# Token sums as products with a column of ones, and scales spread by products with the identity, in a two-block sequence kernel

## The chip, the core and the metric

One NeuronCore of a Trainium2 chip runs the whole program in one launch. The metric is the device time of that launch in microseconds (us), the median of several runs. The kernel before takes 2175.45 us (three runs, 2174.98 to 2176.43). TensorE is called PE below, its weight loads PEld, VectorE DVE, ScalarE ACT and GpSimd POOL; SP issues most DMAs.

## The reference, cut to what matters

Two blocks follow each other on 1024 tokens of 1024 features. The change touches the normalizations only. Each is

```
def rms_norm(x, w):
    xf = x.astype(jnp.float32)
    y = xf * lax.rsqrt(jnp.mean(xf * xf, axis=-1, keepdims=True) + EPS)
    return (y * w.astype(jnp.float32)).astype(x.dtype)
```

and they stand before the first block's input product, before its gate, at its end, before the second block's input product, after its mixer, before its feed-forward part and after it. Besides them a modulation vector `mod = silu(c) @ ada_w + ada_b` of 6 x 1024 numbers is made, by the same sum over partitions.

## The kernel before, in words

Features lie on the 128 partitions, tokens along the free axis, in two halves of H = 512 tokens. Matrix products are done on PE in float32r with each operand split in a high and a low part, so each product of 128 x 128 weights with 512 tokens is three PE instructions (`mm3`). PE's order is the order in which the program is written: `tick` counts the modelled time of these products, and every 2500 ns (640 ns in the feed-forward part) `slot` lets generators on the lists `fast` and `side` take one step, so a `yield` in a generator puts the next PE instructions that many slots later. On DVE, ACT, POOL and SP a scheduler orders the instructions.

A norm is a chain over engines. While the features come out of their products, ACT squares them and DVE adds the eight squares up in an accumulator of 128 x 512 (`acc`). What is left is a sum over the 128 partitions for each token, and a scale for each token that must stand on all partitions.

- `token_sums` (line 2539 before) has PE transpose the accumulator in chunks of 128 tokens into PSUM (one instruction for each chunk, `tr`, line 2478), and DVE sums along the free axis (line 2545). The result is a column for each chunk: token on the partition.
- `rsqrt_cols` (line 2549) scales on DVE and raises to the power -0.5 on POOL (line 2552).
- `to_rows` (line 2554) has DVE multiply the identity by the repeated columns (line 2557, 128 x 512, into a tile `C` or `B`), PE multiplies a 128 x 128 tile of ones with it (one product of 512 float32 columns, two PE instructions), and ACT copies the result out of PSUM.

`token_sums` is called 27 times: twice in phase A (`rstd`), twelve times for the modulation vector (`ada`, line 1557), twice for the gate's norm, four times in `norms` (two norms for each half: the first block's last and the second's first, lines 1710 and 1711), four times in `mid` and three times in `finish` (512, 256 and 256 tokens). That is 104 chunks. `to_rows` is called 15 times, 56 chunks. In `norms` the second scale is computed from the first: `r1`, then `r2` by three small products, a second power and a last product (lines 1712 to 1718). `norms(0)` is followed by the scaling of the second block's inputs (`x1`), which DVE and ACT do between the last drains of the gate products; `mid(1)` makes the feed-forward inputs of the second half while the products of the first half run; `finish` ends the program.

Of the kernel before, what the change touches and what calls it, by code (L numbers as in the profile page):

```python
# [8 lines left out]
F32 = mybir.dt.float32  # L9
# [3 lines left out]
ALU = mybir.AluOpType  # L13
# [3 lines left out]
P = 128  # L17
T = 1024
H = 512
D = 1024  # L20
NCH = T // P
EPS = 1e-6
# [98 lines left out]
class PhaseA:  # L121
# [14 lines left out]
    def phase_a(self):  # L136
        nc, tc = self.nc, self.tc
# [18 lines left out]
        acc = tp.tile([P, NCH * 256], F32, tag="vt", name="acc_a", bufs=1)[:, :T]  # L156
        rb = tp.tile([P, T], F32, tag="rb", name="rb_a")
        rt = sp.tile([P, NCH], F32, tag="rt", name="rt_a")
        rtmp = sp.tile([P, NCH], F32, tag="rtmp", name="rtmp_a")
# [3 lines left out]
        for half in range(2):  # L163
            hs = slice(half * H, half * H + H)
# [24 lines left out]
        def rstd(half):  # L189
            hs = slice(half * H, half * H + H)  # L190
            hr = slice(half * 4, half * 4 + 4)
            self.token_sums(rt[:, hr], acc[:, hs])
            self.rsqrt_cols(rt[:, hr], rt[:, hr], 1.0 / D, EPS, rtmp[:, hr])
            yield
            yield
            self.to_rows(rb[:, hs], rt[:, hr], 4)
# [24 lines left out]
        for k in range(8):  # L221
            first_k(p0, 0, k)
        p1 = {j: self.sm_ps() for j in range(3)}
        chain = rstd(0)
        for k in range(8):
            first_k(p1, 1, k)
            if k in (1, 4, 6):
                next(chain, None)
        for j in range(4):
            drain(p0[j], first[j], 0)  # L230
        p1[3] = self.mm_ps()
        chain = rstd(1)
        for k in range(8):
            first_k({3: p1[3]}, 1, k)
# [1293 lines left out]
class PhaseC:  # L1528
# [11 lines left out]
    def ada(self, g, half, pool):  # L1540

        o = g * 1024 + half * H
        for k in range(8):
            raw = pool.tile([P, H], F32, tag="adar", name=self.name("adar"), bufs=2)
            self.nc.sync.dma_start(raw, self.a["adaw"][k * P : k * P + P, o : o + H])
            if k == 0:
                acc = pool.tile([P, H], F32, tag="adaa", name=self.name("adaa"), bufs=1)
                self.ts(acc, raw, self.cact[:, 0:1])
            else:
                self.stt(acc, raw, self.cact[:, k : k + 1], acc, ALU.mult, ALU.add)  # L1550
            if k % 2:
                yield
        yield
        yield
        j = g * 8 + half * 4
        m = self.mods[:, j : j + 4]
        self.token_sums(m, acc)
        self.add(m, m, self.col("ada_b_2", j, 4))

    def halves(n, head, tail):  # L1560

# [12 lines left out]
    def rstd_rows(self, sums, col, tmp, rows, lag=3, res=None):  # L1574

        n = sums.shape[1] // P
        self.token_sums(col, sums)
        self.rsqrt_cols(col, col, 1.0 / D, EPS, tmp)
        for _ in range(lag):
            yield  # L1580
        r = self.to_rows(rows, col, n)
        if res is not None:
            res.append(r)

    def phase_c(self, yh, yl):
        nc, tc = self.nc, self.tc
        tp = tc.alloc_tile_pool(name="tc", bufs=1, side="left")
        sp = tc.alloc_tile_pool(name="tcs", bufs=1, side="left")
        br = self.br = tc.alloc_tile_pool(name="bridge", bufs=1, side="right")
# [5 lines left out]
        def B_():  # L1595
            return br.tile([P, H], F32, tag="B", name=self.name("B"), bufs=3)
# [3 lines left out]
        def pair(pool, n):  # L1600
            return [pool.tile([P, H], F32, tag=f"{n}{j}", name=self.name(n)) for j in range(2)]
# [9 lines left out]
        acc, rb = pair(tp, "acc"), pair(tp, "rb")  # L1611
        rt = br.tile([P, NCH], F32, name="rt_c")
        rtmp = br.tile([P, NCH], F32, name="rtmp_c")
# [50 lines left out]
        for n, (m, half) in enumerate(self.UC[6:]):  # L1664
            ps = self.mm_ps()
# [8 lines left out]
        acc1, acc2 = pair(br, "acc1"), pair(br, "acc2")  # L1674
# [15 lines left out]
            accum(acc2[half], m, hh, scale=self.col("final_norm_w", m))  # L1690


        wfa = br.tile([P, 8], F32, name="wfa")
        r1 = br.tile([P, NCH], F32, name="r1")
        r2 = br.tile([P, NCH], F32, name="r2")
        rb12 = pair(br, "rb12")
        self.x2d = [tc.dram_tile([P, T], F32, name=f"x2d{k}") for k in range(8)]
        x1 = self.x1 = []
# [1 line left out]
        def norms(half):  # L1700
            if not x1:

                self.stt(wfa, self.mods[:, 8:16], 1.0, self.col("pre1_w_2", 0, 8), ALU.add, ALU.mult)
                self.mul(wfa, wfa, self.col("final_norm_w", 0, 8))
                x1.extend(self.moving())
            hs = slice(half * H, half * H + H)
            hr = slice(half * 4, half * 4 + 4)
            for _ in range(4):
                yield
            self.token_sums(r1[:, hr], acc1[half])  # L1710
            self.token_sums(r2[:, hr], acc2[half])
            self.rsqrt_cols(r1[:, hr], r1[:, hr], 1.0 / D, EPS, rtmp[:, hr])
            self.mul(r2[:, hr], r2[:, hr], r1[:, hr])
            self.mul(r2[:, hr], r2[:, hr], r1[:, hr])
            self.rsqrt_cols(r2[:, hr], r2[:, hr], 1.0 / D, EPS, r2[:, hr])
            self.mul(r2[:, hr], r2[:, hr], r1[:, hr])
            yield
            yield
            self.to_rows(rb12[half], r2[:, hr], 4)
            for k in range(8):  # L1720
                t = B_()
                s = self.mods[:, k : k + 1]
                self.stt(t, h[k][:, hs], wfa[:, k : k + 1], rb12[half], ALU.mult, ALU.mult)
                self.act(x1[0][k][half], t, AF.Identity, bias=s)
                self.stt(x1[1][k][half], t, s, x1[0][k][half].bitcast(F32), ALU.add, ALU.subtract)

        def store_x2(half):
            hs = slice(half * H, half * H + H)
            if half == 0:
                for _ in range(4):  # L1730
                    yield
            rb1 = br.tile([P, H], F32, tag=f"acc1{half}", name=self.name("rb1"))
            self.to_rows(rb1, r1[:, half * 4 : half * 4 + 4], 4)
            for k in range(8):
                t = B_()
                self.stt(t, h[k][:, hs], self.col("final_norm_w", k), rb1, ALU.mult, ALU.mult)
                (nc.sync if k % 2 else nc.gpsimd).dma_start(self.x2d[k][:, hs], t)
                yield

        def chain():  # L1740
            yield from norms(1)
            yield from store_x2(0)
            yield from store_x2(1)
# [6 lines left out]
        for m, half in self.UG[6:]:  # L1750
            ps = self.mm_ps()
            self.prod(ps, ws.get(("g", m)), x, half)
            gate_drain(ps, m, half)
            if (m, half) == (7, 0):
                self.drain_side()
                self.fast.append(norms(0))
# [579 lines left out]
class K(PhaseA, PhaseB, PhaseC, PhaseF):  # L2336
# [199 lines left out]
        nc.gpsimd.memset(self.mhalf, -0.5)  # L2536


    def token_sums(self, out, acc):

        n = out.shape[1]
        ps = self.sm_ps()[:, : n * P]
        for j in range(n):
            self.tr(ps[:, j * P : (j + 1) * P], acc[:, j * P : (j + 1) * P])
        self.nc.vector.tensor_reduce(
            out=out, in_=ps.rearrange("p (n c) -> p n c", n=n), axis=mybir.AxisListType.X, op=ALU.add
        )

    def rsqrt_cols(self, out, src, scale, eps, tmp):

# [2 lines left out]

    def to_rows(self, out, colt, n):

        dg = self.C_().rearrange("p (n c) -> p n c", n=4)[:, :n, :]
        self.nc.vector.tensor_tensor(
            out=dg, in0=self.ident.unsqueeze(1).broadcast_to([P, n, P]), in1=colt.unsqueeze(2).broadcast_to([P, n, P]),
            op=ALU.mult,
        )  # L2560
        ps = self.sm_ps()[:, : n * P]
        self.mm(ps, self.ones, dg.rearrange("p n c -> p (n c)"))
        if out is None:
            return ps
        self.act(out, ps, AF.Copy)
# [26 lines left out]
```

## Time and profile before

| what | value |
|---|---|
| median of three runs | 2175.45 us |
| the profiled execution | 2174.98 us, its span 2173.3 us |
| granted clock of PE, mean | 0.994 |
| PE busy | 2127.4 us (98%) |
| DVE busy | 1505.0 us (69%) |
| ACT busy | 904.7 us (42%) |
| POOL busy | 120.5 us (6%) |

The page's busy time of PE holds the modelled ends of pipelined products, so the start of one product to the start of the next is read instead where a cost is wanted. A line of a timeline is: start, length of the merged run, engine, line, operation, result and operands, shape, count, and in brackets the idle time before it with what ended it.

### The profile page before, as it was taken

How to read it: one execution, taken by the hardware profiler on the slowest of the kernel's cores; microseconds unless marked ns; L12 is line 12 of the kernel's file. 1: busy time of each engine (PE TensorE's matmuls, PEld its weight loads, DVE VectorE, ACT ScalarE, POOL GpSimd, SP SyncE). 2: the span in 40 equal slices, each digit the busy share in tenths (PEclk: the TensorE clock that was granted, in tenths of full speed). 3: DMA queues.
4: the chain of work that ended last, by engine and by line, in shares of the span. 5: the costliest groups of instructions: out<-in, count | busy, mean ns of one | idle time of the engine just before them, and what ended most of it. 6: DMA issues, size and time to landing. Idle time of an engine off the chain costs nothing.

```text
span 2173.3 us, 29295 instructions
## 1 busy us (share of the span) xinstructions
PE 2127.4 (98%) x10998; PEld 1763.7 (81%) x10998; DVE 1505.0 (69%) x2338; ACT 904.7 (42%) x1522; POOL 120.5 (6%) x210
## 2 busy tenths in 40 slices
PE   8999999999999999999999999999899999999997
PEld 7988888887799898787887778887688888878886
DVE  7575687676576633558766345848988776769988
ACT  5554453343345544525253222446523223234443
POOL 1000000000212110000000000001000000000000
PEclk9999999999999999999999999999999999999998
DMA  5111115421363334346555355654342222258645
GB/s 179 30 42 32 51 30 188 142 78 37 119 210 120 104 107 147 129 152 207 170 183 144 128 197 181 197 170 166 122 150 93 87 88 88 73 194 293 199 163 165
DMA packets 146150, 290.76 MB, mean 134 GB/s; under 512 B 21184, under 2 KB 43600, under 8 KB 145752
## 3 DMA queue, kind: packets, MB, share of 16 engines
q1 hardware_dynamic: 131464, 264.51, 37.4%
q0 software_dynamic: 8128, 20.07, 2.7%
q10 hardware_dynamic: 6416, 4.31, 0.7%
q8 instruction: 87, 1.43, 0.3%
q14 instruction: 55, 0.45, 0.1%
HBM read 225.74 MB, written 61.90 MB: 132 GB/s over the span
## 4 chain that ended last, share of the span: by engine, by line
PE 85%; DVE 8%; DMA 2%; issue 2%; ACT 2%; POOL 0%; SPq 0%; POOLq 0%; DVEq 0%; ACTq 0%
PE mm L2469 63%; PE sm L2469 21%; PE sm L2478 1%; DVE lo L2437 1%; DVE res L2437 1%; DVE res L2449 1%; DMA mD<-mlrows 1%; DVE rl L2449 0%; DVE B L2449 0%; ACT C L2463 0%; DVE rl L2437 0%; DVE tv L2437 0%; DVE acc L2437 0%; ACT T L2463 0%; ACT hi L2463 0%
## 5 line engine op out<-in xcount | busy, mean ns | idle before, releaser
L2469 PE MATMUL mm<-rh,hi 128*128 128x512 f32 x1552 | 623.9, 402 | 3.3 <-DVE c L2437 2.3
L2469 PE MATMUL mm<-rh,lo 128*128 128x512 f32 x1552 | 606.2, 391 | 0.0
L2469 PE MATMUL mm<-rl,hi 128*128 128x512 f32 x1552 | 605.3, 390 | 0.0
L2469 PEld LDWEIGHTS mm<-rh,hi 128*128 128x128 f32 x1552 | 291.9, 188 | 73.8 <-issue 8.3
L2469 PEld LDWEIGHTS mm<-rh,lo 128*128 128x128 f32 x1552 | 291.6, 188 | 62.3
L2469 PEld LDWEIGHTS mm<-rl,hi 128*128 128x128 f32 x1552 | 292.2, 188 | 59.4 <-issue 3.1
L2463 ACT ACTIVATE hi<-raw 128x1024 fp32r<-128x1024 f32 (+2 forms) x189 | 183.0, 971 | 372.7 <-PE mm L2469 271.7
L2437 DVE TENSOR_TENSOR lo<-raw,hi 128x1024 fp32r<-128x1024 f32 (+2 forms) x189 | 209.9, 1113 | 94.2 <-ACT hi L2463 92.4
L2469 PE MATMUL mm<-yr,hi 128*128 128x512 f32 x384 | 118.6, 390 | 0.9 <-ACT yr L2463 0.7
L2469 PE MATMUL mm<-hi,rh 128*128 128x256 f32 (+1 forms) x384 | 110.7, 288 | 0.0
L2469 PE MATMUL mm<-hi,rl 128*128 128x256 f32 (+1 forms) x384 | 109.2, 284 | 0.0
L2469 PE MATMUL mm<-lo,rh 128*128 128x256 f32 (+1 forms) x384 | 109.2, 284 | 0.0
L2469 PE MATMUL mm<-tv,hi 128*128 128x512 f32 x312 | 99.6, 399 | 3.5 <-ACT tv L2463 2.0
L2449 DVE SCALAR_TENSOR_TENSOR adaa<-adar,cact,adaa 128x512 f32<-128x512 f32 x84 | 62.9, 749 | 37.5 <-DMA adar<-in_adaw 36.7
L2469 PEld LDWEIGHTS mm<-yr,hi 128*128 128x128 f32 x384 | 72.1, 188 | 16.5 <-ACT yr L2463 1.1
L2463 ACT ACTIVATE hi<-sl 128x512 fp32r<-128x512 f32 x66 | 39.1, 627 | 107.4 <-PE sm L2469 72.5
L2469 PEld LDWEIGHTS mm<-tv,hi 128*128 128x128 f32 x312 | 59.9, 192 | 18.4 <-DVE tv L2437 3.1
L2469 PEld LDWEIGHTS mm<-hi,rh 128*128 128x128 f32 x384 | 73.4, 191 | 1.6 <-issue 1.2
L2469 PE MATMUL mm<-yr,lo 128*128 128x512 f32 x192 | 74.7, 389 | 0.0
L2469 PEld LDWEIGHTS mm<-hi,rl 128*128 128x128 f32 x384 | 73.4, 191 | 0.7 <-issue 0.2
L2469 PEld LDWEIGHTS mm<-lo,rh 128*128 128x128 f32 x384 | 73.4, 191 | 0.0
L2469 PE MATMUL sm<-tv,hi 128*128 128x512 f32 x216 | 66.5, 389 | 0.0
(521 smaller groups left out, 3905.7 us busy)
## 6 DMA issues: line engine op xcount, KB each, us to landing
raw<-in_w SPq DMA_DIRECT2D x60, 512.0 KB
adar<-in_adaw SPq DMA_DIRECT2D x96, 256.0 KB
raw<-in_wfo SPq DMA_DIRECT2D x40, 512.0 KB
c<-ffa SPq DMA_DIRECT2D x69, 256.0 KB
raw<-in_wfi SPq DMA_DIRECT2D x30, 512.0 KB
raw<-in_wo SPq DMA_DIRECT2D x24, 512.0 KB
ru<-in_wfi SPq DMA_DIRECT2D x22, 512.0 KB
raw<-in_wpj SPq DMA_DIRECT2D x32, 256.0 KB
```

What stands on the lines that cost most here:

```text
L2437: self.nc.vector.tensor_tensor(out=out, in0=a, in1=b, op=op)
L2449: self.nc.vector.scalar_tensor_tensor(out=out, in0=a, scalar=s, in1=b, op0=op0, op1=op1)
L2463: self.nc.scalar.activation(out=out, in_=a, func=f, scale=scale, **kw)
L2469: self.nc.tensor.matmul(out, lhsT=l, rhs=r, start=start, stop=stop)
L2478: self.nc.tensor.transpose(out, a, self.ident[:n, :n])
```

## The change

`token_sums` becomes one product for each chunk, with the chunk of the accumulator as the weights and a single column of ones as the moving operand; the sums arrive in PSUM as columns, and DVE reads them there in its next instruction, so the reduction on DVE is gone. `to_rows` becomes one product for each chunk, with the column repeated 128 times (a stride of zero) as the weights and the identity as the moving operand; the DVE multiplication and its tile are gone. `norms` computes both scales from the two sums at once: `1/r2^2` is `sum2/D + EPS*(sum1/D + EPS)` up to the factor that the last product held, and one power over 8 columns stands for two over 4 one after the other.

```diff
         def rstd(half):
-            self.token_sums(rt[:, hr], acc[:, hs])
-            self.rsqrt_cols(rt[:, hr], rt[:, hr], 1.0 / D, EPS, rtmp[:, hr])
+            self.rsqrt_cols(rt[:, hr], self.token_sums(acc[:, hs]), 1.0 / D, EPS, rtmp[:, hr])
...
-        self.token_sums(m, acc)
-        self.add(m, m, self.col("ada_b_2", j, 4))
+        self.add(m, self.token_sums(acc), self.col("ada_b_2", j, 4))
...
-            self.token_sums(r1[:, hr], acc1[half])
-            self.token_sums(r2[:, hr], acc2[half])
-            self.rsqrt_cols(r1[:, hr], r1[:, hr], 1.0 / D, EPS, rtmp[:, hr])
-            self.mul(r2[:, hr], r2[:, hr], r1[:, hr])
-            self.mul(r2[:, hr], r2[:, hr], r1[:, hr])
-            self.rsqrt_cols(r2[:, hr], r2[:, hr], 1.0 / D, EPS, r2[:, hr])
-            self.mul(r2[:, hr], r2[:, hr], r1[:, hr])
-            yield
-            yield
-            self.to_rows(rb12[half], r2[:, hr], 4)
+            ps = self.sm_ps()[:, :8]
+            for q, sums in enumerate((acc1, acc2)):
+                self.token_sums(sums[half], ps[:, 4 * q : 4 * q + 4])
+            self.ts(t12[:, 0], ps[:, 0:4], 1.0 / D, EPS)
+            self.ts(t12[:, 1], t12[:, 0], EPS)
+            self.stt(t12[:, 1], ps[:, 4:8], 1.0 / D, t12[:, 1], ALU.mult, ALU.add)
+            nc.gpsimd.tensor_tensor(
+                out=r12[half].rearrange("p q n -> p (q n)"), in0=t12.rearrange("p q n -> p (q n)"), in1=self.mhalf, op=ALU.pow
+            )
+            yield
+            yield
+            self.to_rows(rb12[half], r12[half][:, 1], 4)
...
-    def token_sums(self, out, acc):
-        n = out.shape[1]
+    def token_sums(self, acc, out=None):
+        n = acc.shape[1] // P
+        if out is None:
+            out = self.sm_ps()[:, :n]
+        for j in range(n):
+            self.mm(out[:, j : j + 1], acc[:, j * P : (j + 1) * P], self.ones[:, 0:1])
+        return out
...
         ps = self.sm_ps()[:, : n * P]
         for j in range(n):
-            self.tr(ps[:, j * P : (j + 1) * P], acc[:, j * P : (j + 1) * P])
-        self.nc.vector.tensor_reduce(
-            out=out, in_=ps.rearrange("p (n c) -> p n c", n=n), axis=mybir.AxisListType.X, op=ALU.add
-        )
...
-        dg = self.C_().rearrange("p (n c) -> p n c", n=4)[:, :n, :]
-        self.nc.vector.tensor_tensor(
-            out=dg, in0=self.ident.unsqueeze(1).broadcast_to([P, n, P]), in1=colt.unsqueeze(2).broadcast_to([P, n, P]),
-            op=ALU.mult,
-        )
-        ps = self.sm_ps()[:, : n * P]
-        self.mm(ps, self.ones, dg.rearrange("p n c -> p (n c)"))
+            self.mm(ps[:, j * P : (j + 1) * P], colt[:, j : j + 1].broadcast_to([P, P]), self.ident)
```

On PE every instruction keeps its place. On the other engines the scheduler's order moves with the removed rows. On DVE in `norms(0)` (`acc` is an accumulator of squares, `sm` a PSUM bank, `C<-mm,rb` the drain of a gate product, `C<-ident,r` the multiplication for the spread), before:

```order
L2545 TENSOR_REDUCE r_3507<-sm_4321 128x4
L2545 TENSOR_REDUCE r_3508<-sm_4327 128x4
L2455 TENSOR_SCALAR rtmp_c<-r_3507 128x4
L2437 TENSOR_TENSOR r_3508<-r_3508,r_3507 128x4 x2
L2437 TENSOR_TENSOR C_4359<-mm_4302,rb_2794 128x512
L2455 TENSOR_SCALAR r_3508<-r_3508 128x4
L2437 TENSOR_TENSOR lo_4355<-raw_4353,hi_4354 128x1024
L2437 TENSOR_TENSOR r_3508<-r_3508,r_3507 128x4
L2449 SCALAR_TENSOR_TENSOR C_4359<-C_4359,sm_4346 128x512
L2449 SCALAR_TENSOR_TENSOR res_2789<-C_4359,res_2789 128x512
L2557 TENSOR_TENSOR C_4383<-ident,r_3508 128x512
```

and now:

```order
L2454 TENSOR_SCALAR t_3506<-sm_4318 128x4
L2452 TENSOR_SCALAR t_3506<-t_3506 128x4
L2448 SCALAR_TENSOR_TENSOR t_3506<-sm_4318,t_3506 128x4
L2436 TENSOR_TENSOR C_4350<-mm_4299,rb_2794 128x512
L2436 TENSOR_TENSOR lo_4346<-raw_4344,hi_4345 128x1024
L2448 SCALAR_TENSOR_TENSOR C_4350<-C_4350,sm_4337 128x512
L2448 SCALAR_TENSOR_TENSOR res_2789<-C_4350,res_2789 128x512
```

The two reductions, four small rows between the powers and the multiplication for the spread are gone; the drain stands behind three small rows. On DVE in the second norm of `mid(1)` (`sl`, `sp` and `lo` belong to the feed-forward part's weights and products), before:

```order
L2545 TENSOR_REDUCE rt_f<-sm_13502 128x4
L2437 TENSOR_TENSOR sl_13476<-sl_13476,raw_13384 128x512
L2449 SCALAR_TENSOR_TENSOR sp_12745<-C_13484,sp_12745 128x512
L2455 TENSOR_SCALAR rtmp_f<-rt_f 128x4
L2437 TENSOR_TENSOR sl_13476<-sl_13476,raw_13441 128x512
L2437 TENSOR_TENSOR lo_13525<-sl_13476,hi_13524 128x512
L2437 TENSOR_TENSOR sp_12747<-sm_13511,sp_12746 128x512
L2437 TENSOR_TENSOR lo_13525<-sl_13476,hi_13524 128x512
L2557 TENSOR_TENSOR C_13548<-ident,rt_f 128x512
```

and now:

```order
L2454 TENSOR_SCALAR rtmp_f<-sm_13483 128x4
L2436 TENSOR_TENSOR sl_13457<-sl_13457,raw_13365 128x512
L2448 SCALAR_TENSOR_TENSOR sp_12726<-C_13465,sp_12726 128x512
L2436 TENSOR_TENSOR sl_13457<-sl_13457,raw_13422 128x512
L2436 TENSOR_TENSOR lo_13505<-sl_13457,hi_13504 128x512
L2436 TENSOR_TENSOR sp_12728<-sm_13491,sp_12727 128x512
L2436 TENSOR_TENSOR lo_13505<-sl_13457,hi_13504 128x512
```

The row that POOL waits for stands where the reduction stood, three rows earlier than it did, and the multiplication that PE waited for is gone.

## Rows read from the trace of the kernel before

**Rows 1.** The page, part 1: busy time and share of the span of each engine.

```profile
PE 2127.4 (98%) x10998; PEld 1763.7 (81%) x10998; DVE 1505.0 (69%) x2338; ACT 904.7 (42%) x1522; POOL 120.5 (6%) x210
```

**Rows 2.** The page, part 4: the chain that ended last, by engine.

```profile
PE 85%; DVE 8%; DMA 2%; issue 2%; ACT 2%; POOL 0%; SPq 0%; POOLq 0%; DVEq 0%; ACTq 0%
```

**Rows 3.** Transposes: timeline of PE in phase A, and line 2478 (ns min/median/max).

```profile
35.85 0.60 PE L2478 MATMUL sm<-ident,acc_a 128*128 128x128 f32 x4
...
L2478 PE MATMUL sm<-ident,adaa x48: 270/272/273, 365.0 to 1106.7; 128*128 128x128 f32 x48
```

**Rows 4.** Float32 products of 128 columns: timeline of PE, and their group by shape.

```profile
89.79 1.72 PE L2469 MATMUL sm<-vt,res 128*128 128x128 f32 x14
...
L2469 PE MATMUL sm<-vt,res 128*128 128x128 f32 x56 | 6.9, 275 | 0.0
```

**Rows 5.** A spread: timeline of PE, and the tile of ones (ns min/median/max).

```profile
46.54 1.02 PE L2469 MATMUL sm<-C,ones 128*128 128x512 f32 x2
...
L2469 PE MATMUL sm<-C,ones x18: 590/592/697, 46.5 to 1539.4; 128*128 128x512 f32 x18
```

**Rows 6.** Timeline of PEld: weight loads of sixteen transposes with four columns.

```profile
1139.58 0.57 PEld L2478 LDWEIGHTS sm<-ident,mq 4*128 4x128 f32 x8
1140.08 0.57 PEld L2478 LDWEIGHTS sm<-ident,mD 4*128 4x128 f32 x8
```

**Rows 7.** Groups of PEld by shape (partitions*columns): busy us, mean ns of one.

```profile
L2469 PEld LDWEIGHTS sm<-vt,res 128*128 128x128 f32 x56 | 6.9, 191 | 0.3
L2469 PEld LDWEIGHTS sm<-D,D 128*64 128x64 f32 x128 | 6.8, 136 | 2.0 <-issue 1.1 <-ACT res L2463 0.7
L2478 PEld LDWEIGHTS sm<-ident,adaa 128*128 128x128 f32 x48 | 6.0, 140 | 1.5
L2469 PEld LDWEIGHTS sm<-wc,bb 128*16 128x16 f32 x64 | 5.5, 96 | 1.9 <-issue 1.3
```

**Rows 8.** Lines 2545, 2557 and 2552: ns min/median/max of the removed rows' groups.

```profile
L2545 DVE TENSOR_REDUCE mods<-sm x12: 680/688/693, 365.6 to 1107.9; 128x4 f32<-128x512 f32 x12
L2557 DVE TENSOR_TENSOR C<-ident,rt_f x7: 424/686/704, 1458.8 to 2162.5; 128x512 f32<-128x512 f32 x5, 128x256 f32<-128x256 f32 x2
L2552 POOL TENSOR_TENSOR r<-r,mhalf x2: 1008/1460/1912, 523.5 to 549.5; 128x4 f32<-128x4 f32 x2
```

**Rows 9.** Timeline of PE: spreads that PE waited for, and two products ahead of one.

```profile
525.13 0.39 PE L2469 MATMUL mm<-rl,hi 128*128 128x512 f32 x1
525.36 0.39 PE L2469 MATMUL mm<-rh,lo 128*128 128x512 f32 x1
527.58 1.13 PE L2469 MATMUL sm<-C,ones 128*128 128x512 f32 x2 [1.83 <-DVE C L2557]
563.81 1.12 PE L2469 MATMUL sm<-B,ones 128*128 128x512 f32 x2 [0.45 <-DVE B L2557]
1486.65 1.10 PE L2469 MATMUL sm<-C,ones 128*128 128x512 f32 x2 [0.26 <-DVE C L2557]
1538.91 1.12 PE L2469 MATMUL sm<-C,ones 128*128 128x512 f32 x2 [1.11 <-DVE C L2557]
```

**Rows 10.** Timeline of PE: the first transpose of `norms(1)`.

```profile
545.61 0.30 PE L2478 MATMUL sm<-ident,acc 128*128 128x128 f32 x1 [1.22 <-DVE acc L2437]
```

**Rows 11.** The waits of PE: us in total, times, longest.

```profile
PE sm L2478 <- DVE kd L2437: 0.8, 1, 0.8
```

**Rows 12.** Stretches: their us, busy us of PE, PEld, DVE, ACT, POOL, PEclk, DMA, GB/s.

```profile
1508.00:1580.00 72.00, 64.48 (x253) 49.45 (x252) 71.54 (x115) 42.73 (x71) 6.38 (x9) 0.93 0.35 117
...
1136.00:1142.00 6.00, 6.00 (x44) 4.94 (x44) 5.96 (x7) 5.63 (x7) 0.00 (x0) 1.00 0.47 147
```

**Rows 13.** The program's end: timelines of PE and of DVE.

```profile
2160.32 0.69 PE L2478 MATMUL mm<-ident,acc 128*128 128x128 f32 x2 [4.48 <-DVE acc L2437]
2162.97 1.22 PE L2469 MATMUL mm<-C,ones 128*128 128x256 f32 x2 [1.96 <-DVE C L2557]
...
2162.49 0.43 DVE L2557 TENSOR_TENSOR C<-ident,rt_f 128x256 f32<-128x256 f32 x1 [0.81 <-POOL rt_f L2552]
```

More of the change, by code (lines that the diff above doesn't have):

```diff
@@ L1576, in rstd_rows @@
         n = sums.shape[1] // P
-        self.token_sums(col, sums)
-        self.rsqrt_cols(col, col, 1.0 / D, EPS, tmp)
+        self.rsqrt_cols(col, self.token_sums(sums), 1.0 / D, EPS, tmp)
         for _ in range(lag):
@@ L1693, in phase_c @@
         wfa = br.tile([P, 8], F32, name="wfa")
-        r1 = br.tile([P, NCH], F32, name="r1")
-        r2 = br.tile([P, NCH], F32, name="r2")
+        r12 = [br.tile([P, 2, 4], F32, name=f"r12{j}") for j in range(2)]
+        t12 = br.tile([P, 2, 4], F32, name="t12")
         rb12 = pair(br, "rb12")
@@ L1706, in norms @@
             hs = slice(half * H, half * H + H)
-            hr = slice(half * 4, half * 4 + 4)
             for _ in range(4):
                 yield
-            self.token_sums(r1[:, hr], acc1[half])
-            self.token_sums(r2[:, hr], acc2[half])
-            self.rsqrt_cols(r1[:, hr], r1[:, hr], 1.0 / D, EPS, rtmp[:, hr])
-            self.mul(r2[:, hr], r2[:, hr], r1[:, hr])
-            self.mul(r2[:, hr], r2[:, hr], r1[:, hr])
-            self.rsqrt_cols(r2[:, hr], r2[:, hr], 1.0 / D, EPS, r2[:, hr])
-            self.mul(r2[:, hr], r2[:, hr], r1[:, hr])
+            ps = self.sm_ps()[:, :8]
[7 more added lines that the diff above has]
+            )
             yield
             yield
-            self.to_rows(rb12[half], r2[:, hr], 4)
+            self.to_rows(rb12[half], r12[half][:, 1], 4)
             for k in range(8):
@@ L1732, in store_x2 @@
             rb1 = br.tile([P, H], F32, tag=f"acc1{half}", name=self.name("rb1"))
-            self.to_rows(rb1, r1[:, half * 4 : half * 4 + 4], 4)
+            self.to_rows(rb1, r12[half][:, 0], 4)
             for k in range(8):
```

## The prediction

> **What bounds the kernel now.** I read the page first: PE is busy 98% of the span, DVE 69%, POOL 6% [rows 1], and the chain that ended last lies on PE for 85% [rows 2]. So what the change adds to PE counts nearly in full, and what it takes from DVE counts only where PE waits for DVE. Then I read the timeline of PE at the operations that change, for their prices [rows 3 to 5], the weight loads by shape [rows 6, 7], since the new sums are little but weight loads, and last the waits of PE that a removed DVE row ended [rows 9 to 13]. The sum is made against the profiled execution, 2174.98 us, which is the lowest of the three runs and 0.5 us below their median.
>
> **The token sums on PE.** Four transposes last 0.60 us, one alone 0.272, so one follows another after (0.60 - 0.27) / 3 = 0.109 us [rows 3]. A float32 product is two instructions, each with a weight load of its own: the spread of 512 columns shows as x2, and its second starts (1.02 - 0.59) = 0.43 us after the first [rows 5]. The new sum is such a product with one moving column, so each chunk is two weight loads of 128 columns and two instructions that stream next to nothing. No row has that shape. Fourteen float32 instructions of 128 columns follow each other after (1.72 - 0.275) / 13 = 0.111 us [rows 4], but there load and stream are equally long, and the row doesn't say which sets the pace. The load does, by its lengths: 96 ns for 16 columns, 136 for 64, 191 for 128, a slope of (191 - 96) / 112 = 0.85 ns for a column, thus 0.109 us for 128 columns behind a fixed part that can overlap; a transpose's load of the same 128 columns takes 140 only [rows 7], so its columns go in about twice as fast. The bounds: sixteen loads of transposes with four columns come 0.50 us apart for eight, 0.0625 us each [rows 6], which is the low end if the new loads are like a transpose's; the high end is a load that overlaps with nothing, 0.191 us [rows 7]. I take 0.112 us, nearest to the slope and to the 128-column row. The Trainium skill, "TensorE: Matmul & The Clock Gate", section "LDWEIGHTS (loading the stationary operand)", states that a load takes its columns divided by 1.2 GHz whatever the rows, 0.107 us here. By that rule the sum would be 1 us less; the transposes in rows 6 run against it, the slope in rows 7 agrees.
>
> 104 chunks change; two run at the very end (below). The other 102 cost 102 x (2 x 0.112 - 0.109) = **+11.7 us**. With 0.0625 it would be +1.6, with 0.191 +27.8.
>
> **The spreads on PE.** Four chunks before: two instructions of 0.43 us. After: eight of 0.111. Per chunk 0.222 against 0.214, and 54 chunks without the last two: **+0.5 us**. That the weights repeat one column changes nothing that a row shows.
>
> **What DVE, POOL and the queues lose or gain.** A reduction takes 0.69 us, the multiplication for a spread 0.69 [rows 8]; 27 and 15 of them are some 28 us off DVE, of which PE sees only its waits:
> - `norms(0)`: PE started the spread at 527.58, 1.99 us later than the 0.23 us after the row ahead that products keep [rows 9]. Two reductions (1.4 us), a second power (1.91 there, [rows 8]) and the multiplication (0.69) leave that chain; two longer sums (0.9) and a power over 8 columns instead of 4 enter it, so the scale is ready before PE comes. But behind it DVE runs without a pause to the last gate drain, which PE awaits at 545.61 [rows 10]: what PE wins at 527 it waits there in part. I count **-1.5** of 2.0.
> - the first spread of `store_x2` at 563.81: 0.45 and the 0.16 that a product's length of 0.39 lies over the 0.23 [rows 9]: **-0.6**. The second spread of `mid(0)` at 1486.65, likewise: **-0.4**.
> - the eight modulation sums between 893 and 1107: one wait of 0.8 for DVE, at 1009 [rows 11], should close, PE coming later and DVE having less to do: **-0.8**. The work lies beside PE else and gains nothing.
> - `mid(1)` and the first feed-forward groups, 1508 to 1580: DVE is busy 71.5 of 72.0 us and PE 64.5 [rows 12]; there DVE is the bound. One reduction and one multiplication leave it, about 0.6 us each in a full queue, and the second norm's longer sum and spread on PE (0.5) are covered by PE's waits: **-1.7**. The wait of 1.1 us at 1538.91 [rows 9] goes too, but lies inside this stretch. If DVE were not full there, the 0.5 would come back.
> - the end: DVE's reduction (0.42, by half the columns) and multiplication (0.43, [rows 13]) leave the last chain with about 0.05 of hand-over each, 0.95 in all; against it four loads at half the clock, where two transposes took 0.69, about 0.35 more: **-0.6**.
>
> POOL loses two powers, and the scheduler swaps two loads of `ada_w` with one another's neighbours on SP and sets some ACT splits behind `mid`'s; nothing waits on these by any row read, so they are costed at nothing, and an order that fits less well is kept in the range with 1.5 us to either side. No wait is added: DVE's first row after a sum waits for PE as the reduction did, with the same rows queued behind.
>
> Sum: 11.7 + 0.5 - 1.5 - 0.6 - 0.4 - 0.8 - 1.7 - 0.6 = **+6.6 us**, 2174.98 + 6.6 = **2181.6 us**, slower by 0.3%.
>
> **Rivals.**
> 1. *Loads as fast as a transpose's* (not slower). The pace of a pass is 0.0625 us, not 0.112. For it: sixteen such loads of 128 columns stand in the trace. Against: those are transposes, and rows 7 show other float32 loads half again as long. It decides where a pass is below about 0.08 us: 102 x (2 x 0.08 - 0.109) = 5.2 is what the waits give back. Sum 6.6 - 10.1 = -3.5: 2171.5 us. The Trainium skill, same page, section "Back-to-back issue gap", gives about 25 ns for a matmul of 1 to 64 columns. By that a sum would cost less than half of its transposes, 102 x (0.05 - 0.109) = -6.0, and the time would be 2163.9; no row here has an unpaired load so short.
> 2. *More is absorbed.* The modulation sums' 8 x 0.46 = 3.7 us on PE fall into waits on DVE and ACT that a later PE shortens, and all of the 2.0 at 527 is won. For it: the generators go by PE's time, DVE has slack. Against: the waits between 893 and 1107 are small [rows 11]. Sum 6.6 - 2.9 - 0.5 = +3.2: 2178.2 us.
> 3. *Loads that don't overlap*, 0.191 us: 6.6 + 16.1 = +22.7, 2197.7 us. Against: rows 6 and 4 both show loads closer than their length. A clock that falls in the sums is no better founded: 24 products of four columns between 1136 and 1142 left it at 1.00 [rows 12].
>
> **Chances.** Forecast 0.6, rival 1 0.2 (0.03 of it as far down as the page's figure), rival 2 0.15, rival 3 0.05. A measurement of this kernel can tell about 0.2%, 4.4 us, from no change: faster is below 2171.1, slower above 2179.8. Rival 1 lies on the lower bound, so 0.12 of it is faster and 0.08 the same; rival 2 is the same with 0.13; the forecast, with 1.5 us for the order and 2 for the absorbed waits, gives 0.13 the same and the rest slower. So 0.12 faster, 0.34 the same, 0.54 slower. Range: the forecast's own, 2178 to 2185.5, widened down over rivals 2 and 1 to **2171.0**, and up to **2186.0**; rival 3 and what lies below rival 1 are left out, under 0.2.
>
> **What would show it.** Right: new loads of a sum some 0.11 us apart, a sum of four chunks 0.9 us from its first instruction to the next product, PE's waits at the spreads of `norms(0)` and `mid(1)` gone, DVE's busy time 25 us or more lower, the end 0.5 us shorter from the last square to the first output row. Wrong: sums with passes of 0.06 us or less, or one instruction for a chunk; a fall of PE's clock behind them; or PE's gain at 527 in full and no wait at 545.

## The result and the profile after

The changed kernel takes 2189.23 us in the median of four executions (2187.64 to 2190.18), the kernel before beside it 2175.94 (2174.98 to 2178.34): a ratio of 1.0052, 95% interval 1.0039 to 1.0065. In the later comparisons the kernel before had medians from 2177.6 to 2178.9 in 11 to 26 executions each, so its profiled execution (2174.98) lies at the fast end of a spread from 2174.6 to 2184.2, and the change costs 10 to 13 us, about 11. The forecast was +6.6 us, 2181.6 us, with an upper end of 2186.0: the side was right, the size too small.

The profiled execution of the changed kernel is the slowest of its four, 2190.18 us, 15.2 more than that of before. Page, span and part 1:

```profile
span 2188.4 us, 29626 instructions
...
PE 2142.9 (98%) x11184; PEld 1787.5 (82%) x11184; DVE 1481.6 (68%) x2292; ACT 905.6 (41%) x1522; POOL 118.4 (5%) x208
```

Against [rows 1] DVE lost 23 us of work, and PE gained 15. What a sum and a spread cost shows in PE's timeline, a sum in phase C and the spread of `norms(0)`, each with its neighbours:

```profile
411.88 0.39 PE L2468 MATMUL mm<-rh,lo 128*128 128x512 f32 x1
412.11 0.94 PE L2468 MATMUL sm<-ones,acc 128*128 128x1 f32 x8
412.91 0.49 PE L2468 MATMUL mm<-rh,hi 128*128 128x512 f32 x1
...
529.52 0.39 PE L2468 MATMUL mm<-rh,lo 128*128 128x512 f32 x1
529.75 1.05 PE L2468 MATMUL sm<-ident,r 128*128 128x128 f32 x8
530.55 0.48 PE L2468 MATMUL mm<-rh,hi 128*128 128x512 f32 x1
```

The group of the sums' weight loads by shape (busy us, mean ns of one, idle):

```profile
L2468 PEld LDWEIGHTS sm<-ones,adaa 128*128 128x128 f32 x96 | 12.5, 191 | 0.9
```

Here a pass is one PE instruction with its weight load; a float32 product is two. Eight passes of one column last 0.94 us, one alone 0.16 to 0.25; in the trace's starts they are 0.112 us apart (the first two 0.025 to 0.031), the figure forecast, and their loads last 191 ns as in [rows 7], not the 140 of a transpose. A sum puts the next product 0.46 us later than transposes did. The spread comes 0.23 us after the product ahead of it and nothing waits: the 1.99 us of [rows 9] are gone. The end reads as forecast too (timeline of PE):

```profile
2171.34 0.28 PE L2468 MATMUL sm<-ah,lo 128*128 128x256 f32 x1
2176.09 1.01 PE L2468 MATMUL mm<-ones,acc 128*128 128x1 f32 x4 [4.48 <-DVE acc L2436]
2178.13 1.22 PE L2468 MATMUL mm<-ident,rt_f 128*128 128x128 f32 x4 [1.03 <-POOL rt_f L2550]
```

From the last sum to the spread it is 2.04 us, in [rows 13] 2.65. So the missing microseconds lie elsewhere. I paired each product of after with the same one of before and read how much later it starts. Of the later starts, three stretches hold what the forecast did not have.

**Near 1040.** The waits of PE and of ACT in the changed kernel between 1027 and 1051 (us in total, times, longest):

```profile
PE sm L2468 <- DVE P L1206: 1.6, 1, 1.6
...
ACT e L2462 <- DMA kt<-z_gr: 4.4, 1, 4.4
```

SP's timeline there (start, length, queue):

```profile
1034.09 0.38 SPq L1544 DMA_DIRECT2D adar<-in_adaw  x1
1034.52 0.46 SPq L1301 DMA_DIRECT2D kt<-z_gr  x1
```

Two stretches (columns as in [rows 12]):

```profile
1046.00:1049.00 3.00, 1.41 (x17) 1.21 (x18) 3.00 (x6) 1.15 (x2) 0.00 (x0) 1.00 0.86 261
1049.00:1053.00 4.00, 4.00 (x15) 3.10 (x12) 3.78 (x7) 0.69 (x1) 0.00 (x0) 0.57 0.56 190
```

SP has the load of `kt` behind one more load of `ada_w`, which waits for a buffer that DVE must free. Before, that load stood behind `kt`, by SP's timeline:

```profile
1026.04 0.42 SPq L1302 DMA_DIRECT2D kt<-z_gr  x1
1027.75 6.86 SPq L1545 DMA_DIRECT2D adar<-in_adaw  x4
```

ACT waits 4.4 us for `kt` (0.8 before), DVE's `P` comes late, PE stands, and then runs at a granted clock of 0.57 for 4 us, the lower of the clock's two levels (1.2 instead of 2.4 GHz) for most of them. From 1034 to 1052 PE loses 4.0 us, one sum's 0.46 among them.

**`mid(1)`.** Timelines of SP, of ACT's queue and of DVE, first of the changed kernel, then of the kernel before:

```profile
1570.65 3.43 SPq L1820 DMA_DIRECT2D raw<-in_wfi  x2
...
1574.36 0.33 ACTq L2070 DMA_DIRECT2D uz<-sp  x1
...
1550.07 0.69 DVE L2436 TENSOR_TENSOR lo<-sl,hi 128x512 fp32r<-128x512 f32 x1 [0.72 <-ACT hi L2462]
...
1569.94 0.68 DVE L2436 TENSOR_TENSOR s<-raw,ru 128x512 f32<-128x512 f32 x1
...
1578.51 0.69 DVE L2436 TENSOR_TENSOR rl<-res,rh 128x512 fp32r<-128x512 f32 x1 [1.17 <-DMA uz<-sp]
```

```profile
1541.29 18.39 SPq L1821 DMA_DIRECT2D raw<-in_wfi  x2
...
1561.76 0.33 ACTq L2071 DMA_DIRECT2D uz<-sp  x1
...
1540.56 0.71 DVE L2437 TENSOR_TENSOR s<-raw,ru 128x512 f32<-128x512 f32 x1
1541.16 1.43 DVE L2449 SCALAR_TENSOR_TENSOR res<-res,c,rb 128x512 f32<-128x512 f32 x2
...
1564.64 0.69 DVE L2437 TENSOR_TENSOR rl<-res,rh 128x512 fp32r<-128x512 f32 x1
```

Without the multiplication the scheduler put DVE's `s<-raw,ru`, which frees a tile for a load of weights, behind the scalings of `mid(1)` (`res<-res,c,rb`). Before, it stood ahead of them, and one of two loads of 512 KB went out at 1541, the other at 1559. Now both go out just ahead of the store `uz`; the store lands 4.1 us after its issue, where under 2.9 sufficed before, and DVE waits. DVE also waits 0.72 us for ACT's `hi`, up to 1550.07. Between the same DVE rows, 1528 and 1592 of before, DVE ends 1.1 us later, though it has 1.2 us less to do there.

**`norms(1)`.** In the profiled execution nothing shows, but in a second one (`again`, below) PE's timeline behind the wait for `acc` reads:

```profile
545.89 0.39 PE L2468 MATMUL mm<-rh,lo 128*128 128x512 f32 x1
547.50 1.92 PE L2468 MATMUL sm<-ones,acc 128*128 128x1 f32 x16 [1.22 <-DVE acc L2436]
```

And the stretches behind it:

```profile
549.00:550.00 1.00, 1.00 (x7) 0.92 (x7) 0.41 (x3) 0.00 (x0) 0.00 (x0) 1.00 0.05 13
550.00:554.00 4.00, 4.00 (x12) 3.09 (x12) 0.08 (x1) 0.00 (x0) 1.64 (x1) 0.57 0.00 0
554.00:560.00 6.00, 6.00 (x32) 5.09 (x31) 1.83 (x3) 3.44 (x6) 0.00 (x0) 1.00 0.00 0
```

After the wait and 1.8 us of passes of one column the granted clock falls to its lower level for most of the 4 us, and PE loses 1.6 us by it.

### The profile page after: what moved, and what is told of

Read it like the earlier page. It is cut to its first block, busy times and chain, and to the rows that moved or that the text cites. A ratio compares the mean times of both kernels' runs of the same rounds, so it can differ in the third digit from the quotient of the medians.

```text
span 2188.4 us, 29626 instructions
## 1 busy us (share of the span) xinstructions
PE 2142.9 (98%) x11184; PEld 1787.5 (82%) x11184; DVE 1481.6 (68%) x2292; ACT 905.6 (41%) x1522; POOL 118.4 (5%) x208
## 4 chain that ended last, share of the span: by engine, by line
PE 84%; DVE 7%; DMA 4%; issue 3%; ACT 2%; SPq 0%; POOL 0%; POOLq 0%; DVEq 0%; ACTq 0%
PE mm L2468 62%; PE sm L2468 21%; DVE lo L2436 1%; PE sm L2477 1%; DMA adar<-in_adaw 1%; DMA mD<-mlrows 1%; DVE res L2448 1%; DVE res L2436 1%; DVE adaa L2448 0%; DVE rl L2448 0%; ACT C L2462 0%; DMA s5y<-s5d 0%; DVE B L2448 0%; ACT T L2462 0%; DMA lam<-in_s5l 0%
```

## The experiments

A granted clock, a wait or a loss is quoted from the profile of the run, which is one execution. Medians are of the run and, in brackets, of the kernel before beside it; behind them stand the ratio and its 95% interval.

**The change again.** No edit.

> The changed kernel a second time, to see which of the waits that are new in its first profile belong to the program. New there: PE waits 2.3 us for a split of s5y at 836 (1.2 before), 1.6 us for P at 1048 with the clock at half behind it until 1053, and 1.2 us of DVE for the store uz at 1577. Theory A (an SP queue in another order): the wait at 1048 comes again, since SP has the load of kt behind one more load of ada_w, and costs 3 to 4 us with the clock; the one at 836, where SP's order is the same as before, and the one at 1577 are landings of transfers and need not come again. Theory B (PE is simply later or earlier by the sums): all three come again at the same size. Theory C (chance): none of the three. Time by A and B 2189, by C some 2182 to 2185 in the median.

2188.65 us (2178.42), ratio 1.0043, 1.0032 to 1.0055. The wait for `P` came again, with 0.4 us and no fall of the clock; DVE waited for `uz` again, 1.3 us; the wait for a split of `s5y` did so in part, and PE's loss there is -0.1 to 2.7 us in profiles with and without the sums, so that one is chance. Theory A had the second wrong: `uz` belongs to the program.

**The parts.** `sums_only`: sums as after, `to_rows` and the two powers as before. `rows_only`: `to_rows` alone as after.

```diff
-            self.token_sums(r1[:, hr], acc1[half])
-            self.token_sums(r2[:, hr], acc2[half])
+            s1, s2 = self.token_sums(acc1[half]), self.token_sums(acc2[half])
```

> The token sums as products with a column of ones, the spreads and the two norms' powers as before. SP's order is that of the changed kernel. Theory A (two weight loads of 0.111 us for a chunk, and SP's order): 11.5 us for the sums, 3 to 4 for kt's load, less 1 to 2 at the norms and in mid(1), so 2188 to 2190, as slow as the whole change. Rival (the spreads on PE are what costs): within 2 us of before.

> The kernel before with only the spreads as products of a repeated column with the identity; sums, powers, places of tiles and SP's order as before. Theory A: +0.5 on PE; from the four waits that a multiplication ended, 1.2 of 2.0 in norms(0), 0.6 in store_x2, 0.4 in mid(0), and 0.4 at the end: 2 to 2.5 us less than before, 2175 to 2176.5. Rival (a second power and reductions still set those waits): 2177 to 2178.5.

`sums_only` 2189.8 (2178.42), 1.0044, 1.0032 to 1.0057: the sums alone cost what the change costs. `rows_only` 2177.68 (2178.35), 0.9993, 0.9983 to 1.0002: at most 2 us to win, by its median less than theory A had. In its profile the spread of `norms(0)` wins 1.9 us, of which the waits behind it take 1.4 back, and DVE waits 1.4 us for `uz`.

**The norms without the sums, and cheaper sums.** `rows_norm`: transposes and reductions as before, else as after. `f32r`: the accumulators written in float32r, with two columns of ones.

```diff
-            self.mm(out[:, j : j + 1], acc[:, j * P : (j + 1) * P], self.ones[:, 0:1])
+            self.mm(out[:, 2 * j : 2 * j + 2], acc[:, j * P : (j + 1) * P].bitcast(F32R), self.onesr)
```

> The spreads as products of a repeated column with the identity, and one power for both norms; the token sums as before, by transposes and a reduction on DVE. SP's order is that of before. Theory A: +0.5 for the spreads, -1 to -2 at the spread of norms(0), -0.6 in store_x2, -0.4 in mid(0), -0.4 at the end, so 2172 to 2175, no slower than before, and no wait of PE for P near 1040. Rival (the spreads cost on PE, or any change of DVE's rows upsets mid(1) and the ada stretch by several us): 2178 or more.

> The changed kernel with the accumulators written in float32r (each partial sum rounded to it), so that a chunk's sum is one weight load and one instruction of two columns in place of two and two. SP's and ACT's order are those of the changed kernel. Theory A: a pass takes about 0.11 us, a sum of four chunks 0.45 instead of 0.89, so 11 to 11.7 us less than the changed kernel: 2177 to 2178.5; the wait for P near 1040 stays. Rival (the sums' price is not the loads; the waits and the clock behind them are): 2184 or more.

Both missed every expectation: 2205.9 and 2211.32 (2178.42). Every product of 512 columns that has its weights in the ring was slower, at a mean granted clock of 0.994, as before. The ring is the set of tiles that hold the products' weights in turn; each of the two kernels had put small tiles ahead of it. The next three take that away, or do it alone.

**The same with every tile in its place; a pad.** `f32r_same` makes the column of ones in place, `rows_norm_same` sums into the tiles of before, `pad32` is the kernel before with

```diff
+        self.pad = b.tile([P, 8], F32, name="pad")
+        nc.vector.memset(self.pad, 0.0)
```

> As f32r (sums in float32r, one weight load and one instruction for a chunk), but the column of ones in float32r is made in place, so that every tile lies where it lies in the changed kernel; in f32r a tile of its own had shifted the weight ring by 32 bytes, and all products of 512 columns followed each other after 233 ns instead of 227. Theory A (the shift made f32r slow; the sums' price is two loads): products at 227 ns again, a sum of four chunks 0.45 us, 2176.5 to 2179.5, within 2 us of before. Rival (float32r sums themselves slow the kernel): above 2200 again. Rival (waits, not loads, make the change slow): 2185 to 2190.

> As rows_norm (spreads on PE and one power for both norms, sums by transposes and reduction), with the sums in the tiles of before, so that the weight ring lies where it does before; in rows_norm it lay 128 bytes further and products took 232 ns. Theory A: products at 227 ns, 2 to 5 us less than before by the waits at the norms, in mid(1) and at the end: 2173 to 2176.5 against 2178.4. Rival (spreads on PE give nothing back): 2178 to 2180. Rival (not the place of the ring): above 2200 again.

> The kernel before with one unused tile of 32 bytes for each partition ahead of the weight ring, as f32r had it by its column of ones. Theory A (the place of the weight tiles sets the pace of products): 233 ns for a product of 512 columns instead of 227, 2205 to 2215. Rival (something else in f32r and rows_norm did it): 2178, products at 227 ns.

`pad32` 2211.83 (2177.63), 1.0156, 1.0142 to 1.0171. Its granted clock is 0.996. In its timeline of PE six products start between 1750.04 and 1751.44, 0.233 us apart, where before has 0.227:

```profile
1750.04 0.63 PE L2469 MATMUL mm<-tv,hi 128*128 128x512 f32 x2
1750.50 0.40 PE L2469 MATMUL mm<-tv,lo 128*128 128x512 f32 x1
1750.73 0.63 PE L2469 MATMUL mm<-tv,hi 128*128 128x512 f32 x2
1751.20 0.40 PE L2469 MATMUL mm<-tv,lo 128*128 128x512 f32 x1
1751.44 0.63 PE L2469 MATMUL mm<-tv,hi 128*128 128x512 f32 x2
```

`f32r_same` 2177.87 (2177.63), 0.9999, 0.9989 to 1.0008: one load and one instruction for a chunk, instead of two of each, take the 11 us away. Its sum in phase C, by PE's timeline:

```profile
409.46 0.50 PE L2467 MATMUL sm<-ones,acc 128*128 128x2 f32 x4
409.83 0.49 PE L2467 MATMUL mm<-rh,hi 128*128 128x512 f32 x1
```

Its waits of PE from 1016 to 1045:

```profile
PE sm L2467 <- DVE P L1206: 4.2, 1, 4.2
```

A sum takes 0.37 us up to the product behind it; PE was 4.2 us ahead of before at 1017 and lost 7 us between 1034 and 1052, in a profile of the slowest of its eleven executions (2182.66). `rows_norm_same` 2174.38 (2177.63), 0.9989, 0.9980 to 0.9998: faster by 3 us, with no load of a float32 sum.

**The order near 1040.** `kt_pool` moves the load into `kt`, the first of each pair of such loads, to POOL's queue; the three `adapool` kernels move the loads of `ada_w` there.

```diff
-                nc.sync.dma_start(grs[h], self.z["gr"][2 * hp + h])
+                (nc.sync if h else nc.gpsimd).dma_start(grs[h], self.z["gr"][2 * hp + h])
```

```diff
-            self.nc.sync.dma_start(raw, self.a["adaw"][k * P : k * P + P, o : o + H])
+            self.nc.gpsimd.dma_start(raw, self.a["adaw"][k * P : k * P + P, o : o + H])
```

> The changed kernel with every second of the loads into kt (that of a head's first half) issued on POOL's queue instead of SP's, so that it no longer stands behind a load of ada_w. Theory A (SP's order costs there): the waits of PE for P between 1044 and 1049 (0.6 us in one profile of the changed kernel, 1.9 in the other with the clock at half behind it) are gone, 0.5 to 3 us less than the changed kernel, 2186 to 2188. Rival (the wait comes from the loads of ada_w, not from kt): same time and the same wait.

> The changed kernel with the loads of ada_w issued on POOL's queue, so that kt, gate_s and the weights no longer stand behind them on SP. In the changed kernel and in f32r_same PE waited for P between 1037 and 1049 (0.4 to 4.2 us, up to 7 us of clock at half behind it); on POOL's queue kt alone (kt_pool) left 0.6. Theory A (SP's new order costs the change some 3 us): PE waits for P no more there, 2184 to 2186.5, 2.5 to 5 us less than the changed kernel (2188.9). Rival (the wait is DVE's, which stands behind rows that wait for ada_w whichever queue loads it): the wait stays, 2187.5 to 2190.

> f32r_same (sums in float32r, each partial sum rounded to it) with the loads of ada_w on POOL's queue. In f32r_same's profile PE was 4.2 us ahead of before at 1017, and lost 7 at 1040 by one wait of 4.2 us for P and 7 us of clock at half. Theory A: that loss goes, 2170 to 2174, faster than before and than rows_norm_same (2174.4). Rival (the wait stays with DVE's rows): 2177 to 2179.

> The control: the kernel before with the loads of ada_w on POOL's queue. Its profile shows no wait of PE for P near 1040. Theory A: nothing to win, 2176.5 to 2178.5. Rival (POOL's queue is better or worse for ada_w in itself): 2 us or more to either side of 2177.6.

`kt_pool` 2185.8 (2177.63), 1.0038, 1.0025 to 1.0052: 3 us less, but PE still waited 0.6 us for `P`, so its gain is not shown to come from there. The other three took 2196.05, 2188.72 and, for the control, 2191.65 (2178.88): POOL's queue costs the kernel before 13 us by itself, so their times tell nothing of the order. Their profiles do. Counted on PE's products, all three issue the load into `kt` within 0.1 us of where the kernel before does, and still PE waited 2.1 and 2.2 us for `P` in `after_adapool` and `f32r_adapool`, and not at all in the control. The place of `kt` on SP alone does not make the wait.

**The sums of `ada`, which alone bring SP's new order.** `f32r_adaold` and `after_adaold` sum in `ada` by transposes, `ada_only` only there by products.

```diff
-        self.add(m, self.token_sums(acc), self.col("ada_b_2", j, 4))
+        ps = self.sm_ps()
+        for i in range(4):
+            self.tr(ps[:, i * P : (i + 1) * P], acc[:, i * P : (i + 1) * P])
...
+        self.add(m, m, self.col("ada_b_2", j, 4))
```

> f32r_same (sums in float32r, each partial sum rounded to it) with the twelve sums of ada as before, by transposes and a reduction. SP's order is then that of before, the load of kt ahead of the load of ada_w again, and PE's work is the same within 0.2 us. Theory A (the order that the ada sums bring costs some 3 us): no wait of PE for P near 1040, 2173 to 2176, against 2177.9 for f32r_same. Rival (the order is free): 2177 to 2179.

> The changed kernel with the twelve sums of ada as before; SP's order is that of before. The sums take back 48 x (2 x 0.112 - 0.109) = 5.5 us of loads. Theory A (the order costs 3 us more): 8.5 us less than the changed kernel's 2188.9, 2179 to 2182. Rival (the order is free): 2182.5 to 2184.5.

> The kernel before with only the twelve sums of ada as products with a column of ones; SP's order is that of the changed kernel. Theory A: 5.5 us of loads and 3 us for the order, with a wait of PE for P near 1040: 2185 to 2188. Rival (the order is free): 2182 to 2184.5.

2175.98, 2186.94 and 2183.87 (2178.35); ratios 0.9986 (0.9976 to 0.9995), 1.0040 (1.0027 to 1.0053) and 1.0026 (1.0016 to 1.0035). By the medians `ada_only` costs its loads, 5.5 us, and nothing for the order, `f32r_adaold` wins 1.9 on `f32r_same`, with intervals that overlap, and `after_adaold` lies above both expectations, 2.0 under the changed kernel where the loads alone are 5.5. The profiles are clearer than the times: all six with SP's new order and the ring in its place have PE waiting for `P` there (0.3, 0.3, 0.4, 1.6, 1.9, 4.2 us), and in three the clock falls behind it; of six with the old order none does. From 1034 to 1052, the sum apart, PE loses 0.7, 0.7, 0.7, 3.5, 3.9 and 7.0 us in those six and at most 0.2 in the others. So the wait goes with the sums of `ada` as products. It is not their length, since in `f32r_same` they take PE no longer than transposes. What is left is the order that they bring and the reductions that DVE no longer does; what of it makes the wait is open. By the times it costs some 0 to 2 us, not the 3 of theory A, and what else `after_adaold` lost is open: its profile, of the slowest of its five executions, has one more pause at 1010 (1.9) and a fall of the clock at 1190 and at 549.

**The spread of `mid(1)`.** `after_mid` is the changed kernel, `best_one` is `f32r_adaold`, each with the multiplication on DVE again for the last norm of `mid(1)`.

```diff
-            yield from self.rstd_rows(acc2[half], rt[:, hr], rtmp[:, hr], rb[1], self.W[4])
+            yield from self.rstd_rows(acc2[half], rt[:, hr], rtmp[:, hr], rb[1], self.W[4], dve=half == 1)
```

> The changed kernel with one spread undone: the last norm's of mid(1) is made by the multiplication on DVE and a product with ones again. In all eight profiles of kernels with that spread on PE, DVE's row that frees a raw tile (s from raw and ru) had moved behind the scalings of mid(1), two loads of weights of 512 KB were issued just ahead of the store uz, and DVE waited 1.1 to 1.5 us for that store; in none of three without it. Theory A (that order turns the gain there into a loss): DVE's wait is gone, PE loses 0.1 to 0.7 between 1515 and 1600 by the timeline of before instead of 1.3 to 2.8, and the time is 1 to 3 us lower, 2186 to 2188 against 2188.9. Rival (the wait is chance): DVE waits for uz again, or the time is 1 us higher for the multiplication.

> f32r_adaold (sums in float32r, each partial sum rounded to it, the sums of ada as before) with the last spread of mid(1) as before; DVE's, SP's and ACT's rows stand in both places in the order of before. Theory A: no wait of PE for P near 1040, none of DVE for uz, and the waits at the norms, in store_x2 and at the end shorter: 2172 to 2175, 1 to 3 us less than f32r_adaold's 2176.0. Rival (the order in mid(1) is free): 2176 to 2178.

`after_mid` 2188.43 (2178.62): DVE's wait for `uz` is gone as theory A had it, but the time is not lower beyond its spread (2187.24 to 2191.21), and PE lost 2.0 us between 1515 and 1600, not 0.1 to 0.7. DVE between the rows at 1528 and 1592 of before ends 0.4 us later instead of 1.1. PE's loss has two parts, which meet at its last wait in the stretch. By PE's timeline, first of before, then of `after_mid`, with a stretch (columns as in [rows 12]) behind it:

```profile
1578.12 0.70 PE L2469 MATMUL mm<-tv,hi 128*128 128x512 f32 x2 [0.92 <-ACT tv L2463]
...
1589.85 0.92 PE L2468 MATMUL mm<-tv,hi 128*128 128x512 f32 x2 [2.47 <-ACT tv L2462]
...
1590.00:1594.00 4.00, 4.00 (x11) 3.12 (x11) 4.00 (x8) 1.51 (x3) 0.00 (x0) 0.57 0.00 0
```

Up to that product PE lost 0.4 us, where the two profiles of the changed kernel lost 1.1 and 1.2: this part follows DVE and its order. The other 1.6 is the clock, which fell right behind the wait. It did so in nine of the 16 profiles with the ring in its place, with either order and for 1.4 to 1.7 us each, but in none of the three whose `mid(1)` is wholly that of before. So this part does not come from the order alone, and why the clock fell in these nine is open. `best_one` 2174.4 (2178.62), 0.9985, 0.9975 to 0.9994: in the range of theory A. Up to the same product PE lost nothing (-0.1, and 0.6 in `f32r_adaold`), and then 1.5 by the clock. Against `f32r_same`, 2177.87, both orders undone give 3.5 us by the medians, though the two intervals just overlap. In the timeline of DVE in `best_one` the row `s<-raw,ru` stands ahead of the scalings again, and nothing waits for the store:

```profile
1539.95 0.68 DVE L2441 TENSOR_TENSOR s<-raw,ru 128x512 f32<-128x512 f32 x1
...
1561.07 1.89 DVE L2441 TENSOR_TENSOR rl<-res,rh 128x512 fp32r<-128x512 f32 x3
1564.08 0.68 DVE L2441 TENSOR_TENSOR rl<-res,rh 128x512 fp32r<-128x512 f32 x1
```

`rows_norm_same` and `best_one` are faster than the kernel before by 3 to 4 us (0.1 to 0.2%), `f32r_adaold` by 2.4; among the three nothing is settled, and only the first keeps the sums in float32.

## Why the prediction was right, and where it failed

- **The token sums, +11.7: right.** Two passes 0.112 us apart for a chunk, by the load's slope in [rows 7] and the pace in [rows 4]. The Trainium skill, "TensorE: Matmul & The Clock Gate", section "LDWEIGHTS (loading the stationary operand)", gives 0.107 for the load, and the trace agrees within 5%; the 25 ns of "Back-to-back issue gap" show once in a sum, between its first two passes (0.025 us at 412.11); behind them every pass comes 0.112 us after the last. Rivals 1 and 3, which stood on the pace, fall. `f32r_same` shows it by time: one load and one instruction less for a chunk are 10.8 us (2188.65 to 2177.87), 10.0 if each is taken against the kernel before beside it.
- **The spreads, +0.5: right.** Eight passes, 0.80 us to the next product; by the paired starts 0.03 more each.
- **The waits that go.** `norms(0)`: forecast -1.5, measured -2.1, and the wait for `acc` behind it stays as long as it was, 1.22 us. That part of the gain would be waited for again was wrong: DVE was earlier by as much as PE. Nor does DVE run "without a pause" there: in the trace of before it waits 0.45, 0.79 and 0.76 us for ACT between 529 and 545, the first time for the spread's own result. `store_x2` -0.7 (forecast -0.6), `mid(0)` -0.4 (-0.4), the end -0.6 (-0.6), the wait for `kd` at 1009 -0.4 (-0.8). But for these two sizes the steps held; DVE's busy time fell by 23 us, not by 25 or more.
- **`mid(1)`, -1.7: the step that failed first.** That DVE is the bound there was right. That two rows less would shorten it, and that the longer sum would be covered by PE's waits, was wrong. The rows did take 1.2 us off DVE's work, but two waits of DVE came in. The one for ACT's `hi` goes with the sum: 0.72 to 0.74 us in the seven profiles with a float32 sum and the ring in its place, 0.3 in the four with float32r, none in the five with transposes. The one for `uz` goes with the order: 1.1 to 1.5 us in all twelve profiles with that spread on PE, none in the seven with the multiplication on DVE. PE lost 1.3 to 2.5 us between 1515 and 1600 in two profiles of the change, 0.8 to 2.1 without the sum that lies there: 2.5 to 3.8 us off the forecast's term. Of this 1.1 and 1.2 lie ahead of PE's last wait at 1578 and are DVE's; the fall of the clock behind it, in one of the two, is the rest.
- **"Nothing waits on these by any row read, so they are costed at nothing": the step that failed second.** The rows that changed places on DVE, SP and ACT were what brought the waits for `uz` and `P`, the first by the row that frees a tile for a load; what brought the second is not found. A row that does not wait in the trace of before is no proof that nothing waits once it stands elsewhere; 1.5 us to either side was too little for three places. Near 1040 this cost 0.7 us in one profile and 3.5 in the other, sums apart.
- **"A clock that falls in the sums is no better founded": wrong.** Of seven profiles with two float32 sums behind the wait in `norms(1)`, five have the clock at its lower level just behind them, for 1.6 us; of the seven with transposes there none has. The passes alone don't do it: the sums of the changed kernel's profile with no wait beside them, over twenty, pass at full clock. The products of four columns in [rows 12] had no wait ahead of them either, so they were the wrong row to judge by.
- **The baseline.** The sum was made against 2174.98. The kernel before has medians of 2175.9 to 2178.9, so some 1 to 4 us of the gap to 2189 were in the start of the sum, not in the change.

Rival 2 (more absorbed) named the wait at 527 rightly and the modulation sums wrongly: each of them costs its full 0.46 us.

## What to carry to other kernels

A float32 product with a moving column is priced by its weight loads, two for 128 columns, 0.11 us each; where PE is the bound, sums by transposes or in float32r (one load for a chunk) are cheaper, and DVE's time saved is worth only what PE waited for. When an edit takes rows out of an engine whose order a scheduler sets, compare the new order of all queues and price each moved row that frees a buffer or issues a load by who waits for what comes behind it. Take a baseline from many executions before you forecast a few tenths of a per cent.

## What the runs showed that was not expected

- Thirty-two bytes ahead of the weight ring (`pad32`) made every product with these weights 0.233 instead of 0.227 us, 128 bytes (`rows_norm`) 0.232, at full clock: 34 us against before, and 31 between `rows_norm` and `rows_norm_same`. Which property of the address does it was not tried; a tile ahead of a tuned ring has to be checked for it.
- The loads of `ada_w` from POOL's queue instead of SP's cost 13 us (`before_adapool`), with new waits of PE at 613 and 1010.
